# Reordering three pieces of work in a hybrid Fourier/SSD encoder layer: the transposed sums of dt, the weighted inputs, the stores of unit outputs

## The chip, the cores and the metric

The kernel runs on one core of one Trainium2 chip. The metric is the time of one execution on the device in microseconds (us). For a kernel that was run several times the median counts; a profiled execution is one more run, with a time of its own.

## The reference, cut to what matters

One encoder layer is computed for two sequences, a prompt of 1024 tokens and a sample of 2048 tokens, with 1024 features each:

```python
u = rms_norm(h, norm_w);  proj = u @ w_in            # 1024 -> 2*512 + 1536 + 2560 + 48
z_f, u_f, z_s, xbc, dt_raw = split(proj)
y_f = (fft2(u_f).real @ w_fmix) * silu(z_f)          # Fourier group
xbc = silu(depthwise_conv5(xbc) + conv_b);  xs, B, C = split(xbc)
dt = softplus(dt_raw + dt_bias)                      # 24 heads forward, 24 backward
a_cs = cumsum(dt * A) in chunks of 128 tokens
y_diag = (C B^T * exp(a_cs[l] - a_cs[s]) masked) @ (xs * dt)      # inside a chunk
states = B^T (xs * dt * exp(a_cs[-1] - a_cs));  scanned over the chunks
y_off  = C @ state_before_chunk * exp(a_cs)          # across chunks
y_s = group_norm((y_fwd + y_bwd + D * xs) * silu(z_s))
h = h + concat(y_f, y_s) @ w_out;  h = h + (p @ w_ple_in) * sigmoid(h @ w_ple_gate)
y = rms_norm(h, final_norm_w)
```

The decay exp(a_cs[l] - a_cs[s]) is needed as a 128 by 128 mask for each chunk, head and direction. To make it, the kernel lays a_cs out as rows, and each row is then loaded into all 128 partitions.

## The kernel before

The tokens are cut into three blocks of 1024: P (the prompt), S1 and S2 (the sample's halves). The first part of the kernel, up to about 1967 us of the profile, does the input projection and the whole SSD work of the three blocks; the Fourier group and the output products come behind it. The change and the prediction concern the first part alone.

**The backbone of the first part** is the projection. Its output is made in jobs of 128 columns (`Job`, line 312). A job has three pieces, one for each third of the block's tokens, and a piece is 24 matmuls on TensorE (line 361): 8 tiles of the contraction, each in three passes, since every operand is held as a rounded part and a rest. Before a job its weights are loaded (`wr`, line 182, one buffer, on the SyncE queue), rounded by ScalarE (`wh`, line 189), and the rest is taken by GpSimd (`wl`, line 190).

**The order of everything else is written out by hand.** `step` (line 286) runs one piece. Ahead of the piece it runs all entries that `pre` has put down for that step, behind it those that `post` has put down, each list in the order in which the entries were registered. Nothing is scheduled beyond that: every engine, and the SyncE queue of DMAs, takes its instructions in the order in which they are written, and waits where an operand is not there. So an entry's step says where it stands on its engine's list, and among entries of one step the order of registration says it. The older unit's entries stand first, since its plan was registered first.

**At the start of a block** the jobs for dt, the first C and the first B run. In steps counted from the block's start, `dt_sums` (line 464, behind step 13) forms the running sums of dt * A with matmuls and copies them to `acs` on ScalarE (line 471). `dt_rows` (line 486, behind step 14) turns `acs` with eight transposes on TensorE into `prw` (line 493); ScalarE copies that to `rows` and takes its exponential, `erow` (lines 494 and 495). `dt_out` (line 498, ahead of step 16) stores both to DRAM, ROWd and EXPd.

**Unit u** is two heads, 128 channels. Its x job starts at step s0, and units of a block follow each other at 9 steps, so three jobs lie between them (the last unit has 6). Unit 0 starts at step 12 of its block. In steps counted from s0, the plan (line 671) says:

- `rows_in` p = 0 to 3 (ahead of steps 4, 6, 8, 10): two DMAs each, which load rows of ROWd into all partitions (`R`, line 540, three buffers for each direction).
- `rows_cut` (ahead of 6, 8, 10, 12): GpSimd masks both `R` (line 548, two instructions). `rows_exp` (ahead of 7, 9, 11, 13): eight exponentials on ScalarE (line 558). `rows_joined` (ahead of 8, 10, 12, 14): two VectorE operations (lines 563 and 564). `diag` (behind 9, 11, 13, 15): the eight matmuls `pd` (line 575).
- `tokens` (behind 7 and 8): transposes of x into `xm` (lines 421 and 423).
- `weighted` (ahead of 8, 9, 10, 11): GpSimd multiplies `xm` by `wd` into `xw` (line 587, two buffers), one instruction for each direction and half. `states` (behind 9, 10, 11, 12): the matmuls `pst` from `xw` (line 607), then VectorE carries the state over four chunks (lines 614 and 618).
- `decays` (ahead of 11 and 13): loads of `er` from EXPd (line 635). `across` (behind 14 and 16): the matmuls `po` (line 649) and four VectorE operations into the output `y`.
- `gated` (ahead of 16 and 18): GpSimd multiplies `y` by `zT` (line 658), and in block S1 makes two products more (lines 662 and 663). `out` (ahead of 17 and 19): the store of `y` to Yd (line 667), in S1 also of `zT` to ZSd (line 669).

So steps 16 to 19 of one unit are steps 7 to 10 of the next. Beside this, from unit 2 on, `weight_sums` (line 193) forms sums of the output weights: GpSimd lines 217 to 222, its loads on line 205 and its stores to WSd on lines 227 to 229, all on the SyncE queue. While blocks P and S1 run, the next block's tokens are loaded nine times in pieces `xt` for their norm (line 122), which ScalarE squares (line 719).

Of the kernel before, what the change touches and what calls it, by code (L numbers as in the profile page):

```python
# [56 lines left out]
def tile_hybrid_encoder(ctx: ExitStack, tc: tile.TileContext, a):  # L57
# [37 lines left out]
    def bcast_rows(src, n):  # L95
        return src.partition_broadcast(n)
# [5 lines left out]
    with ExitStack() as ph:  # L102
# [63 lines left out]
        def dt_weights_in():  # L166
            wdr = sp.tile([P, KT, 64], F32, tag="R1", bufs=3, name="wdr")
            V.memset(wdr, 0.0)
            for d in range(2):
                nc.sync.dma_start(  # L170
                    wdr[:, :, 32 * d:32 * d + 24],
                    w_in[:, C_DT + 24 * d:C_DT + 24 * (d + 1)].rearrange("(k p) c -> p k c", p=P))
            return wdr

        def dt_weights(wdr):
            S.copy(wdt[:, :, 0, :], wdr)
            V.tensor_tensor(wdt[:, :, 1, :], wdr, wdt[:, :, 0, :].bitcast(F32), op=ALU.subtract)
# [100 lines left out]
        def pre(s_, fn, *args):  # L278
            assert s_ >= slot[0], (s_, slot[0])
            before.setdefault(s_, []).append((fn, args))  # L280

        def post(s_, fn, *args):
            assert s_ >= slot[0], (s_, slot[0])
            behind_.setdefault(s_, []).append((fn, args))

        def step(piece=None):
            for fn, args in before.pop(slot[0], []):
                fn(*args)
            if piece is not None:
                piece()  # L290
            for fn, args in behind_.pop(slot[0], []):
                fn(*args)
            slot[0] += 1
# [231 lines left out]
        class Unit:  # L525
# [145 lines left out]
            def plan(self, s0):  # L671

                B, g = self.B, self.g
                self.y, self.xw, self.er, self.H, self.R, self.xm = {}, {}, {}, {}, {}, {}
                if self.u % 3 == 0:
                    for k, s_ in enumerate((1, 3) if g else (4, 5)):
                        post(s0 + s_, group_tokens, B, g, 4 * k)
                    for k, s_ in enumerate((6, 7)):
                        post(s0 + s_, group_cb, B, g, 4 * k)
                for p in range(4):  # L680
                    s_ = s0 + 4 + 2 * p
                    pre(s_, self.rows_in, p)
                    pre(s_ + 2, self.rows_cut, p)
                    pre(s_ + 3, self.rows_exp, p)
                    pre(s_ + 4, self.rows_joined, p)
                    post(s_ + 5, self.diag, p)
                post(s0 + 7, self.tokens, 0)
                pre(s0 + 8, self.weighted, 0, 0)
                post(s0 + 8, self.tokens, 4)
                pre(s0 + 6, self.state_in)  # L690
                pre(s0 + 9, self.weighted, 1, 4)
                post(s0 + 9, self.states, 0, 0)
                pre(s0 + 10, self.weighted, 0, 4)
                post(s0 + 10, self.states, 1, 4)
                pre(s0 + 11, self.weighted, 1, 0)
                post(s0 + 11, self.states, 0, 4)
                post(s0 + 12, self.states, 1, 0)
                for d in (1, 0):
                    pre(s0 + 11, self.decays, d, 0)
                    pre(s0 + 13, self.decays, d, 4)  # L700
                post(s0 + 14, self.across, 0)
                pre(s0 + 16, self.gated, 0)
                pre(s0 + 17, self.out, 0)
                post(s0 + 16, self.across, 4)
                pre(s0 + 18, self.gated, 4)
                pre(s0 + 19, self.out, 4)

        def norm_piece(b, i):

# [14 lines left out]
        def ple_weights():  # L724
            nc.sync.dma_start(PLd, a["w_ple_in"][0].rearrange("(k p) c -> p k c", p=P))
# [36 lines left out]
        def x_in(b, i):  # L762
            xs[b["n"], i] = load_x(b, i)

        def x_norm(b, i):
            x_normed(b, i, xs[b["n"], i])

        def x_turn(b, i):
            x_turned(b, i, xs.pop((b["n"], i)))
# [5 lines left out]
        with tc.manual_schedule():  # L775
            b0 = BLOCKS[0]
            x_in(b0, 0)
            nc.sync.dma_start(nwb, bcast_rows(a["norm_w"][0], P))
            x_in(b0, 1)
            x_in(b0, 2)  # L780
            coming[0].load()
            x_in(b0, 3)
            wdr = dt_weights_in()
            x_in(b0, 4)
            x_norm(b0, 0)
            x_norm(b0, 1)
            x_turn(b0, 0)
            x_norm(b0, 2)
            x_turn(b0, 1)
            coming[0].split()  # L790
            coming[1].load()
            x_in(b0, 5)
            x_norm(b0, 3)
            x_turn(b0, 2)
            dt_weights(wdr)
            coming[1].split()
            pre(0, small_in)
            post(2, small_constants)
            for i in range(3, 9):
                if i > 3:  # L800
                    pre(i - 4, x_norm, b0, i)
                if i > 5:
                    pre(i - 6, x_in, b0, i)
                post(i - 3, x_turn, b0, i)
            pre(9, decay_rates)
            for B, js, what in rows_:
                bi, s0 = B.bi, slot[0]
                if what == "first":
                    q = s0 if bi else s0 + 1
                    post(q + 7, dt_turned, B)  # L810
                    pre(q + 8, dt_softplus, B, 0)
                    pre(q + 9, dt_softplus, B, 1)
                    post(s0 + 13, dt_sums, B)
                    post(s0 + 14, dt_rows, B)
                    pre(s0 + 16, dt_out, B)
                elif what == "last" and bi < 2:
                    b = BLOCKS[bi + 1]
                    for i, s_ in enumerate((2, 3, 4, 4, 5, 6, 8, 9, 10)):
                        pre(s0 + (0, 0, 1, 2, 2, 3, 5, 6, 7)[i], x_in, b, i)
                        pre(s0 + s_ - 1, x_norm, b, i)  # L820
                        post(s0 + s_, x_turn, b, i)
                elif isinstance(what, int):
                    B.units[what].plan(s0)
                    if 2 <= what < 10:
                        weight_sums(8 * bi + what - 2, s0)
                    if what == 3 and bi == 1:
                        ple_weights()
                    if what == 6 and bi < 2:
                        for i in range(9):
                            pre(s0 + 2 * i, norm_piece, BLOCKS[bi + 1], i)  # L830
                for si in range(3):
                    for j in js:
                        step(lambda: j.piece(si))
            while before or behind_:
                step()
# [550 lines left out]
```

## Time and profile before

| what | value |
|---|---|
| median of 3 runs | 3039.06 us (3034.24 to 3042.33) |
| the profiled execution | 3031.59 us, its span 3029.8 us |
| TensorE matmul busy | 2836.0 us, 94% |
| VectorE, ScalarE, GpSimd busy | 2228.9, 1389.1, 1475.5 us |
| mean granted TensorE clock | 0.972 |
| projection matmuls, line 361 | 8640, from 21 to 1967 us |
| DMA | 440.56 MB, mean 145 GB/s |

How to read it: the profile gives one execution, instruction by instruction. A row of a timeline says when an instruction (or a run of like ones) began, how long it took, its engine, line and operands, and in brackets how long its engine had been idle before it and what ended that. A row of the waits sums such idle time by who waited for whom: total, count, longest. A busy TensorE is what one wants here, so idle time in front of its instructions is what can be gained, and idle time on the other engines counts only where TensorE comes to wait for it.

### The profile page before, as it was taken

Reading aid. Unit: us, or ns where it says so; the run is one execution under the profiler, and the core shown is the slowest. Engines: PE = TensorE matmul, PEld = TensorE weight load, DVE = VectorE, ACT = ScalarE, POOL = GpSimd, SP = SyncE. Lnnn points to the kernel's source line nnn. Section 1 sums busy time; section 2 is a strip of 40 time slices with the busy share of each in tenths; the row PEclk is TensorE's granted clock in tenths of the full one; section 3 lists DMA queues with packets and bytes.
Section 4 is the critical chain, followed back from the end, with each engine's and each line's share of the span. In section 5 each row is a group of like instructions: output and inputs, shape, how many; then the busy total and the mean of one; then the engine's idle time right before and its main releaser. Section 6 shows DMA issues by size and latency. Waiting matters only on the chain. (4 is left out here: it accounts for less than half of the span.)

```text
span 3029.8 us, 47051 instructions
## 1 busy us (share of the span) xinstructions
PE 2836.0 (94%) x17252; PEld 2566.2 (85%) x17252; DVE 2228.9 (74%) x3412; ACT 1389.1 (46%) x2980; POOL 1475.5 (49%) x1114
## 2 busy tenths in 40 slices
PE   6899999989999899989999999969999899989998
PEld 6899989988999889989999999957677677768887
DVE  3687767666687568666779787687989988875665
ACT  4444545434544454434544444434433533354554
POOL 1355645431567565642555655455777578610000
PEclk9999999999999999999999999979999999999999
DMA  3378878972588778862677787566554644352221
GB/s 96 76 129 162 158 157 173 139 142 79 125 171 167 152 181 165 154 167 64 127 154 146 159 144 158 117 210 250 173 184 132 236 149 150 133 198 91 94 85 69
DMA packets 454579, 440.56 MB, mean 145 GB/s; under 512 B 24384, under 2 KB 405444, under 8 KB 450508
## 3 DMA queue, kind: packets, MB, share of 16 engines
q1 hardware_dynamic: 454060, 436.50, 60.6%
q8 instruction: 137, 2.24, 0.3%
q14 instruction: 94, 0.77, 0.1%
q10 hardware_dynamic: 288, 1.05, 0.1%
HBM read 328.41 MB, written 110.10 MB: 145 GB/s over the span
## 5 line engine op out<-in xcount | busy, mean ns | idle before, releaser
L361 PE MATMUL ps<-uh,wh 128*128 128x342 f32 (+1 forms) x2880 | 961.6, 334 | 8.4 <-ACT uh L267 8.4
L361 PE MATMUL ps<-ul,wh 128*128 128x342 f32 (+1 forms) x2880 | 926.3, 322 | 2.5 <-DVE ul L268 2.5
L361 PE MATMUL ps<-uh,wl 128*128 128x342 f32 (+1 forms) x2880 | 927.4, 322 | 0.4 <-POOL wl L190 0.4
L190 POOL TENSOR_TENSOR wl<-wr,wh 128x1024 fp32r<-128x1024 f32 x120 | 305.5, 2546 | 707.9 <-ACT wh L189 650.5
L361 PEld LDWEIGHTS ps<-uh,wh 128*128 128x128 f32 x2880 | 552.2, 192 | 20.1 <-ACT uh L267 9.2
L361 PEld LDWEIGHTS ps<-ul,wh 128*128 128x128 f32 x2880 | 554.5, 193 | 4.2 <-DVE ul L268 3.5
L361 PEld LDWEIGHTS ps<-uh,wl 128*128 128x128 f32 x2880 | 550.4, 191 | 1.2 <-POOL wl L190 1.1
L558 ACT ACTIVATE R<-R,lb 128x128 f32<-128x128 f32 x1152 | 356.8, 391 | 98.3 <-POOL R L548 98.2
L548 POOL TENSOR_SCALAR_AFFINE_SELECT R<-R 128x512 f32<-128x512 f32 x288 | 257.5, 905 | 193.7 <-DMA R<-ROWd 187.2
L618 DVE SCALAR_TENSOR_TENSOR H<-H,cd,pst 128x64 f32<-128x64 f32 x888 | 182.6, 274 | 47.7 <-PE pst L607 44.6
L402 DVE SCALAR_TENSOR_TENSOR xT<-raw,cvt,xT 128x1024 f32<-128x1024 f32 x144 | 214.8, 1492 | 2.6
L1102 PE MATMUL X<-whP,ah 128*128 128x512 f32 x480 | 195.2, 407 | 8.0 <-ACT pu L1111 6.4
L1102 PE MATMUL X<-wlP,ah 128*128 128x512 f32 x480 | 193.6, 403 | 1.6 <-DVE wlP L861 1.6
L1102 PE MATMUL X<-whP,al 128*128 128x512 f32 x480 | 192.5, 401 | 2.4 <-DVE al L1073 2.4
L587 POOL TENSOR_TENSOR xw<-xm,wd 128x512 f32<-128x512 f32 x144 | 181.8, 1268 | 18.7 <-PE pst L607 18.5
L367 ACT COPY raw<-ps 128x342 f32<-128x342 f32 x180 | 78.3, 438 | 241.7 <-PE ps L361 226.8
L1214 POOL TENSOR_TENSOR ht<-ht,pu 128x512 f32<-128x512 f32 x96 | 151.9, 1590 | 63.1 <-ACT pu L1111 43.0
L607 PE MATMUL pst<-xw,Bm 128*128 128x128 f32 x1056 | 151.3, 285 | 24.0 <-POOL xw L587 23.8
L607 PEld LDWEIGHTS pst<-xw,Bm 128*128 128x128 f32 x1056 | 131.9, 192 | 41.6 <-POOL xw L587 30.3
L189 ACT CAST wh<-wr 128x1024 fp32r<-128x1024 f32 x120 | 125.8, 1049 | 67.9 <-DMA wr<-in_w_in 67.2
L1073 DVE TENSOR_TENSOR al<-s,ah 128x512 fp32r<-128x512 f32 x144 | 143.6, 1021 | 16.4 <-ACT ah L1072 16.3
L563 DVE TENSOR_TENSOR R<-R,R 128x512 f32<-128x512 f32 x144 | 134.1, 931 | 25.9 <-ACT R L558 23.5
(264 smaller groups left out, 5703.9 us busy)
## 6 DMA issues: line engine op xcount, KB each, us to landing
R<-ROWd SPq DMA_DIRECT2D x288, 256.0 KB
wr<-in_w_in SPq DMA_DIRECT2D x120, 512.0 KB
er<-EXPd SPq DMA_DIRECT2D x288, 128.0 KB
Hd<-ht SPq DMA_DIRECT2D x48, 512.0 KB
ht<-Hd SPq DMA_DIRECT2D x48, 512.0 KB
y<-Yd SPq DMA_DIRECT2D x46, 512.0 KB
wlP<-WSd SPq DMA_DIRECT2D x21, 1024.0 KB
Yd<-y SPq DMA_DIRECT2D x72, 256.0 KB
```

The costliest lines, as they stand in the source:

```text
L190: G.tensor_tensor(wl, raw, wh.bitcast(F32), op=ALU.subtract)
L361: T.matmul(ps[:, :n], lhsT=wt[:, kt, :], rhs=ut[:, kt, :n], start=(i == 0), stop=(i == 3 * KT - 1))
L402: V.scalar_tensor_tensor(dst, raw[:, k:k + TB], cvt[:, 20 * k + ct:20 * k + ct + 1], dst, op0=ALU.mult, op1=ALU.add)
L548: G.affine_select(out=R.rearrange("p c h l -> p (c h) l"), in_=R.rearrange("p c h l -> p (c h) l"), pattern=[[0, 4], [sgn, P]], compare_op ...
L558: S.activation(R[:, c, h, :], R[:, c, h, :], AF.Exp, bias=self.B.lb[:, 2 * p + c, hc + h:hc + h + 1])
L563: V.tensor_tensor(E[0], E[0], E[1], op=ALU.add)
L587: G.tensor_tensor(xw, self.xm[c4].rearrange("p c (h e) -> p c h e", h=2), col(self.B.wd[:, c4:c4 + 4, hc:hc + 2]).broadcast_to([P, 4, 2, 6 ...
L607: T.matmul(pst[:, c, :], lhsT=B.Bm[self.g][:, c4 + c, :], rhs=xw[:, c, :, :].rearrange("p h e -> p (h e)"), start=True, stop=True)
L618: V.scalar_tensor_tensor(dst[:, e], H[d][:, cc, e], B.cd[:, cc, hc + h:hc + h + 1], pst[:, c, e], op0=ALU.mult, op1=ALU.add)
L1073: V.tensor_tensor(al, src, ah.bitcast(F32), op=ALU.subtract)
L1102: T.matmul(ps, lhsT=at[:, k, :], rhs=wt[:, k, :], start=(first and i == 0), stop=(i == 11), skip_group_check=not first)
L1214: return lambda t: G.tensor_tensor(h, h, t, op=ALU.add)
```

## The change

Three things move; no instruction is added or taken away.

1. `dt_rows` goes from behind step 14 of a block to behind step 15. `dt_out` stays ahead of step 16.
2. In a unit's plan the loop over `rows_in`, `rows_cut`, `rows_exp`, `rows_joined` and `diag` is registered behind `tokens`, `weighted`, `states` and `decays` instead of in front of them. Their steps are the same; where both have entries in one step, the order is turned round. On GpSimd `weighted` comes ahead of `rows_cut` in steps 8 and 10; on TensorE `states` ahead of `diag` behind steps 9 and 11.
3. `out` goes from ahead of steps 17 and 19 to ahead of steps 18 and 20.

```diff
@@ plan
                     for k, s_ in enumerate((6, 7)):
                         post(s0 + s_, group_cb, B, g, 4 * k)
-                for p in range(4):
-                    s_ = s0 + 4 + 2 * p
-                    pre(s_, self.rows_in, p)
-                    pre(s_ + 2, self.rows_cut, p)
-                    pre(s_ + 3, self.rows_exp, p)
-                    pre(s_ + 4, self.rows_joined, p)
-                    post(s_ + 5, self.diag, p)
                 post(s0 + 7, self.tokens, 0)
                 pre(s0 + 8, self.weighted, 0, 0)
...
                     pre(s0 + 13, self.decays, d, 4)
+                for p in range(4):
+                    s_ = s0 + 4 + 2 * p
+                    pre(s_, self.rows_in, p)
+                    pre(s_ + 2, self.rows_cut, p)
+                    pre(s_ + 3, self.rows_exp, p)
+                    pre(s_ + 4, self.rows_joined, p)
+                    post(s_ + 5, self.diag, p)
                 post(s0 + 14, self.across, 0)
                 pre(s0 + 16, self.gated, 0)
-                pre(s0 + 17, self.out, 0)
+                pre(s0 + 18, self.out, 0)
                 post(s0 + 16, self.across, 4)
                 pre(s0 + 18, self.gated, 4)
-                pre(s0 + 19, self.out, 4)
+                pre(s0 + 20, self.out, 4)
@@ the block's start
                     post(s0 + 13, dt_sums, B)
-                    post(s0 + 14, dt_rows, B)
+                    post(s0 + 15, dt_rows, B)
                     pre(s0 + 16, dt_out, B)
```

What this does to the lists of three engines, at the places of which the prediction speaks:

ScalarE at the start of block S1, from the sums of dt on; before:

```order
L479 ACTIVATE wd<-wd 128x512
L483 ACT_TABLE_LOAD
L483 ACTIVATE lb<-lb 128x512
L367 COPY raw<-ps 128x342
L494 COPY rows<-prw 64x512
L495 ACT_TABLE_LOAD
L495 ACTIVATE erow<-prw 64x512
L494 COPY rows<-prw 64x512
L495 ACTIVATE erow<-prw 64x512
L189 CAST wh<-wr 128x1024
L406 ACTIVATE xT<-raw,cvt 128x1024
L272 ACTIVATE zT<-ps 128x342 x2
```

The same place after the change:

```order
L479 ACTIVATE wd<-wd 128x512
L483 ACT_TABLE_LOAD
L483 ACTIVATE lb<-lb 128x512
L367 COPY raw<-ps 128x342
L189 CAST wh<-wr 128x1024
L406 ACTIVATE xT<-raw,cvt 128x1024
L272 ACT_TABLE_LOAD
L272 ACTIVATE zT<-ps 128x342
L494 COPY rows<-prw 64x512
L495 ACTIVATE erow<-prw 64x512
L494 COPY rows<-prw 64x512
L495 ACTIVATE erow<-prw 64x512
```

The next job's `wh`, the start of a convolution (`xT`), and the first piece of `zT` now stand in front of the copies of the turned sums. Either list has two loads of an activation table.

GpSimd in unit 3 of block S1, from the masks of step 8 to the inputs of steps 10 and 11; before:

```order
L548 AFFINE_SELECT R_9324<-R_9324 128x512
L548 AFFINE_SELECT R_9326<-R_9326 128x512
L587 TENSOR_TENSOR xw<-xm,wd 128x512
L190 TENSOR_TENSOR wl<-wr,wh 128x1024
L658 TENSOR_TENSOR y<-y,zT 128x512
L662 TENSOR_TENSOR er_9220<-er_9220,elt 128x512
L663 TENSOR_TENSOR zT<-er_9220,zT 128x512
L587 TENSOR_TENSOR xw<-xm,wd 128x512
L548 AFFINE_SELECT R_9450<-R_9450 128x512
L548 AFFINE_SELECT R_9452<-R_9452 128x512
L587 TENSOR_TENSOR xw<-xm,wd 128x512 x2
```

The same place after the change:

```order
L587 TENSOR_TENSOR xw<-xm,wd 128x512
L548 AFFINE_SELECT R_9324<-R_9324 128x512
L548 AFFINE_SELECT R_9326<-R_9326 128x512
L190 TENSOR_TENSOR wl<-wr,wh 128x1024
L658 TENSOR_TENSOR y<-y,zT 128x512
L662 TENSOR_TENSOR er_9212<-er_9212,elt 128x512
L663 TENSOR_TENSOR zT<-er_9212,zT 128x512
L587 TENSOR_TENSOR xw<-xm,wd 128x512 x2
L548 AFFINE_SELECT R_9450<-R_9450 128x512
L548 AFFINE_SELECT R_9452<-R_9452 128x512
L587 TENSOR_TENSOR xw<-xm,wd 128x512
```

The first and the third `xw` of the unit have changed places with a pair of masks each. The second `xw` still has the same instructions in front of it: the pair of masks, the first `xw`, `wl`, and the three products of the unit before (lines 658 to 663).

The SyncE queue in the same unit, between two weight loads `wr`; before:

```order
L182 DMA wr<-in_w_in 128x8x128
L667 DMA Yd_61<-y 128x512
L669 DMA ZSd<-zT 128x512
L540 DMA R_9450<-ROWd_68 128x2x256
L540 DMA R_9452<-ROWd_68 128x2x256
L227 DMA WSd_78<-wb 128x2x256
L228 DMA WSd_78<-wb 128x256
L229 DMA WSd_78<-ws 128x4x256
L205 DMA wb<-in_w_out 128x2x256 x2
L182 DMA wr<-in_w_in 128x8x128
```

The same place after the change:

```order
L182 DMA wr<-in_w_in 128x8x128
L540 DMA R_9450<-ROWd_68 128x2x256
L540 DMA R_9452<-ROWd_68 128x2x256
L227 DMA WSd_78<-wb 128x2x256
L228 DMA WSd_78<-wb 128x256
L229 DMA WSd_78<-ws 128x4x256
L667 DMA Yd_61<-y 128x512
L669 DMA ZSd<-zT 128x512
L205 DMA wb<-in_w_out 128x2x256 x2
L182 DMA wr<-in_w_in 128x8x128
```

The two stores of the unit before now stand behind two loads of `R` and the stores of the weight sums, but still in front of the next weight load `wr`. At step 11 the second pair of stores stands in the same way behind the last pair of `R` loads and in front of the `er` loads.

## The prediction

> **What bounds the kernel now.** I read the page first, then the waits of TensorE, then the timeline of each engine around the longest of them.
>
> ```profile
> span 3029.8 us, 47051 instructions
> PE 2836.0 (94%) x17252; PEld 2566.2 (85%) x17252; DVE 2228.9 (74%) x3412; ACT 1389.1 (46%) x2980; POOL 1475.5 (49%) x1114
> ```
>
> TensorE is busy for 2836.0 of 3029.8 us, and the change takes no work from it. So only its idle time, 194 us, and the time at a low clock can be gained. The waits of TensorE, with total, count and longest, name two that the change is near:
>
> ```profile
> PE pst L607 <- POOL xw L587: 23.8, 18, 3.8
> PE prw L493 <- ACT acs L471: 17.2, 3, 7.6
> PE pd L575 <- ACT wh L189: 10.1, 2, 6.2
> ```
>
> Together 41 us, 1.4% of the span, are the most that parts 1 and 2 can win as waits. The third row matters for part 3, and so do a wait of the SyncE queue and one of ScalarE:
>
> ```profile
> SPq L667 <- POOL y L658: 243.6, 49, 9.5
> ACT xt L719 <- DMA xt<-in_x_sample: 61.0, 15, 9.1
> ```
>
> The queue stands 243.6 us in front of stores whose products GpSimd hasn't made; ScalarE waits 61.0 us for pieces of the next block's tokens.
>
> **Part 1, the transposes a step later.** The three waits are one in each block (P, S1, S2):
>
> ```profile
> 106.36 1.92 PE L493 MATMUL prw<-ident,acs 128*64 128x128 f32 x8 [7.57 <-ACT acs L471]
> 749.76 1.49 PE L493 MATMUL prw<-ident,acs 128*64 128x128 f32 x6 [4.81 <-ACT acs L471]
> 1418.40 0.85 PE L493 MATMUL prw<-ident,acs 128*64 128x128 f32 x3 [4.79 <-ACT acs L471]
> ```
>
> A step's matmuls last about 3.7 us: two groups of transposes with one step between them start 4.2 us apart, and the first takes 0.6.
>
> ```profile
> 760.73 0.60 PE L421 MATMUL ptt<-ident,BT 128*128 128x128 f32 x4
> 764.92 0.60 PE L421 MATMUL ptt<-ident,BT 128*128 128x128 f32 x4
> ```
>
> ScalarE's copy `acs` comes when it came before, so one step put into the wait leaves 3.9, 1.1 and 1.1 us. The clock adds to this. Behind the waits of S1 and S2 the granted clock (third column from the end) was low:
>
> ```profile
> 751.00:757.00 6.00, 6.00 (x29) 5.92 (x28) 1.72 (x3) 5.96 (x9) 0.00 (x0) 0.65 0.00 1
> 1420.00:1426.00 6.00, 6.00 (x28) 6.00 (x27) 1.72 (x3) 5.95 (x10) 0.00 (x0) 0.64 0.00 0
> 785.00:800.00 15.00, 13.23 (x93) 12.57 (x92) 12.27 (x20) 9.16 (x22) 12.31 (x8) 1.00 0.56 94
> 932.00:936.00 4.00, 2.70 (x11) 2.70 (x12) 2.85 (x5) 1.14 (x4) 4.00 (x4) 0.59 1.12 361
> ```
>
> 0.35 of 6 us, 2.1 us, is lost in S1 and as much in S2. The last two rows are for scale: a wait of 1.77 us (row below) left the clock at 1.00, one of 3.77 us (quoted in part 2) took it to 0.59. So 1.1 us should cost no clock, 3.9 us still should. TensorE then stands 3.7 us earlier in P, 3.7 + 2.1 = 5.8 in S1 and S2: 15.3 us. This is the upper bound of part 1.
>
> Not all of it stays, since what unit 0 needs next doesn't move as far. ScalarE in S1 before:
>
> ```profile
> 753.77 0.58 ACT L494 COPY rows<-prw 64x512 f32<-64x512 f32 x1
> 754.35 1.28 ACT L495 ACT_TABLE_LOAD   x1
> 756.60 0.59 ACT L495 ACTIVATE erow<-prw 64x512 f32<-64x512 f32 x1
> 757.09 1.04 ACT L189 CAST wh<-wr 128x1024 fp32r<-128x1024 f32 x1
> 758.03 1.25 ACT L406 ACTIVATE xT<-raw,cvt 128x1024 f32<-128x1024 f32 x1
> 759.18 0.44 ACT L272 ACTIVATE zT<-ps 128x342 f32<-128x342 f32 x1
> ```
>
> Now `wh`, `xT`, a table load and `zT` stand ahead of the rows. From 753.8 on they take 1.04 + 1.25 + 1.28 + 0.44, and rows, erow, rows 0.58 + 0.59 + 0.58: the rows are ready at 759.6, where the last `erow` began behind them at 756.60 before. Before, that readiness was not used, as the queue shows:
>
> ```profile
> 760.64 0.37 SPq L182 DMA_DIRECT2D wr<-in_w_in  x1
> 761.06 1.10 SPq L499 DMA_DIRECT2D ROWd<-rows  x1
> 765.54 3.13 SPq L540 DMA_DIRECT2D R<-ROWd  x4
> ```
>
> The store of ROWd stood behind a weight load that waited for `wl`, hence for `wh`. Now `wh` is 3.2 us earlier, and the store goes at 759.6 instead of 761.06: 1.4 us earlier. Up to 1.5 more may come because that weight load's 512 KB have left the DMA engines by then. I take 2. The loads of `R` follow it, and behind those the next weight load, which ends the chain:
>
> ```profile
> 782.39 0.64 POOL L548 TENSOR_SCALAR_AFFINE_SELECT R<-R 128x512 f32<-128x512 f32 x1 [1.83 <-DMA R<-ROWd]
> 785.62 1.06 ACT L189 CAST wh<-wr 128x1024 fp32r<-128x1024 f32 x1 [4.93 <-DMA wr<-in_w_in]
> 786.81 2.40 POOL L190 TENSOR_TENSOR wl<-wr,wh 128x1024 fp32r<-128x1024 f32 x1 [2.77 <-ACT wh L189]
> 789.16 1.56 POOL L587 TENSOR_TENSOR xw<-xm,wd 128x512 f32<-128x512 f32 x1
> 790.77 1.16 PE L607 MATMUL pst<-xw,Bm 128*128 128x128 f32 x8 [1.77 <-POOL xw L587]
> 144.98 0.71 PE L607 MATMUL pst<-xw,Bm 128*128 128x128 f32 x4 [0.51 <-POOL xw L587]
> 1454.96 1.05 POOL L587 TENSOR_TENSOR xw<-xm,wd 128x512 f32<-128x512 f32 x1
> 1457.30 0.49 PE L607 MATMUL pst<-xw,Bm 128*128 128x128 f32 x3
> ```
>
> DMA to `wh` to `wl` to the second `xw` to `pst`: TensorE already waited here in P and S1, and in S2 it had 1.3 us to spare (1457.30 less 1456.01). So unit 0's second `pst` comes 2 us earlier in P and S1 and 3.3 in S2, 7.3 in all; the rest of the 15.3 turns into a wait for GpSimd there. In S1 that wait is some 5 us and will cost clock, about 1.3 us (the lower clock after 749.76 cost 2.1). Part 1: -6, bounds -15.3 and, if nothing of the chain moves, +1.3.
>
> **Part 2, `weighted` ahead of the masks.** Unit 3 of S1 has the longest of the 18 waits:
>
> ```profile
> 922.30 1.22 POOL L548 TENSOR_SCALAR_AFFINE_SELECT R<-R 128x512 f32<-128x512 f32 x2
> 923.49 1.05 POOL L587 TENSOR_TENSOR xw<-xm,wd 128x512 f32<-128x512 f32 x1
> ...
> 931.22 2.02 POOL L587 TENSOR_TENSOR xw<-xm,wd 128x512 f32<-128x512 f32 x1
> 933.30 2.07 PE L607 MATMUL pst<-xw,Bm 128*128 128x128 f32 x8 [3.77 <-POOL xw L587]
> ```
>
> The rows left out are `wl` and the three products of unit 2; no row of GpSimd here has idle time in brackets, and TensorE waits for the second `xw`. The change only swaps the first `xw` (1.05) with the masks (1.22); the sum in front of the second is the same, so its wait stays. I count 0, with the whole 23.8 as the far end below. What it costs: masks in steps 8 and 10 come 1 to 2 us later, and exponentials, joins and `diag` behind them. They are covered by the step between each of these stages: the long wait of `pd` quoted above names `wh`, not an exponential or a join. +0.5; were the cover gone, 36 units times two masks times 1.05 would be 76 us, which sets no bound worth keeping.
>
> The same product took 1.05 us at 923.49 and 2.02 at 931.22, so a moved `xw` may land beside other VectorE work: 0.97 us more in the eleven later units of S1, +10.7, is the bound above. The Trainium skill (GPSIMD Engine Reference, Specifications) says that GpSimd shares its SBUF interfaces with VectorE, which contends where it reads two inputs from SBUF; by it the swap would give between 0 and that 10.7, and the two durations agree with it.
>
> **Part 3, stores a step later.** In unit 3 of S1 the `R` loads of step 8 stood behind a ZSd store that waited for GpSimd:
>
> ```profile
> 910.56 0.37 SPq L182 DMA_DIRECT2D wr<-in_w_in  x1
> ...
> 922.38 0.33 SPq L669 DMA_DIRECT2D ZSd<-zT  x1
> 922.80 0.93 SPq L540 DMA_DIRECT2D R<-ROWd  x2
> ```
>
> They can now follow the weight load at 910.56, and what stands behind the stores goes up to 3 us earlier, in step 10 likewise; the last of it reaches the `xt` loads, for which ScalarE waits 61.0 us, and behind two of these waits TensorE lost 10.1 us and a low clock. I take 4 of these 10.1, bounds 0 and -13. The buffers of `y` are written again two and four steps after the later stores, which is 8 us or more of cover; without it VectorE would wait for a DMA.
>
> **The sum**, against the profiled execution's own 3031.6 us (span 3029.8 and 1.8 around it): -6 + 0.5 - 4 = -9.5, 3022.1. The three runs' median, 3039.06, lies 7.5 higher; from it the same difference gives 3029.6.
>
> **The rivals.**
>
> *A. The time in unit 0 is not taken back.* If the weight load there lands with TensorE's new place, part 1 keeps its 15.3, and with part 3 at -6 the sum is -21: 3018. Against it speaks the wait 4.93 for that very load.
>
> *B. The waits only move.* If ROWd lands no earlier (its 4.5 us up to the `R` loads grow by what it starts earlier) and the queue is bound by the transfers and not by its waits, what is left is +1 to -3: about 3038. For it speaks that the `R` loads went only at 765.54, behind a store issued at 761.06.
>
> *C. Slower: loads let go early share the DMA engines with a weight load.* In step 8 the pair of `R` loads now follows `wr` at once, where it stood 12 us behind. The four `R` loads issued at 765.54 were there by 782.39, 16.9 us, so a pair takes up to 8.4. If the engines serve both together, `wr` lands up to half of that, 4.2 us, later, and `wh`, `wl` and the second `xw` with it. In the eleven later units of S1 that is +46; less the 9.5, +37: 3076. From 0.9 us of delay a unit it eats the gain. For it: 16.9 us for four loads that the queue issued in 3.13 shows them standing at the engines. Against it: in unit 0, the last `R` was there at 782.39, the weight load behind it at 785.62.
> The Trainium skill (DMA: Bandwidth & Descriptors, Queues, rings and completion order) says that an engine takes the descriptors of a ring in order; by that rule C adds nothing, and the rows of unit 0 agree.
>
> **How the numbers follow.** About 0.3%, 9.1 us, is what a measurement of this kernel tells from no change. Forecast (-14 to -4) 0.46; A 0.20; B 0.21; C 0.13. The forecast straddles the bound: 0.25 of it beyond, 0.21 within. Faster: 0.25 + 0.20 = 0.45; the same: 0.21 + 0.20 of B = 0.41; slower: C and the rest of B, 0.14. The range takes in A to -25 (3014) and at the top +5 (3044), which is part 2 at its bound of cost and a delay of 0.3 us a unit as in C; what is left out is the rest of C and the far ends.
>
> **What would show it.** Right: `prw` waits of about 3.9, 1.1 and 1.1 us; no low clock behind them in S1 and S2; the second `pst` of unit 0 waiting 2 to 5 us; the total of `pst` behind `xw` as large as before or larger; the queue's wait in front of Yd well below 243.6; `xt` waits below 61. Wrong: `pst` waits under 12 us (part 2 or A does more than I think), `wh` waiting longer for `wr` (C), or a new wait of VectorE for a store of `y`.

## The result, and the profile after

| | before | changed |
|---|---|---|
| median, timed side by side | 3040.36 us (3034.24 to 3042.33, 4 runs) | 3018.1 us (3010.3 to 3022.51, 4 runs) |
| ratio, 95% interval | | 0.9927 (0.99 to 0.9955) |
| the profiled execution, its span | 3031.59, 3029.8 us | 3021.5, 3019.7 us |

The change makes the kernel 22 us faster, where 9.5 were forecast. The changed kernel was timed whole in this group of runs alone; in the three later groups the kernel before has medians of 3028.44, 3030.56 and 3030.88 us, so a ratio is taken within a group only. The page of the changed kernel begins:

```profile
span 3019.7 us, 47067 instructions
PE 2831.3 (94%) x17252; PEld 2570.1 (85%) x17252; DVE 2217.9 (73%) x3412; ACT 1389.5 (46%) x2980; POOL 1488.2 (49%) x1114
```

TensorE's idle time fell from 194 to 188 us and its busy time by 4.7, so this one profile explains only 10 of the 22 us. Where it was won and lost shows when the trace is cut at the last projection matmul. Columns from the left: window, its length, busy time of TensorE (and count), weight loads, VectorE, ScalarE, GpSimd, granted clock, DMA share, GB/s. Before:

```profile
0.00:1967.00 1967.00, 1858.83 (x12818) 1786.07 (x12820) 1396.88 (x2338) 918.26 (x2068) 989.08 (x772) 0.98 0.70 141
1967.00:3029.80 1062.80, 977.17 (x4436) 780.10 (x4436) 832.04 (x1074) 470.86 (x913) 486.39 (x342) 0.96 0.45 154
```

Changed:

```profile
0.00:1948.60 1948.60, 1854.44 (x12818) 1789.79 (x12819) 1383.40 (x2338) 919.58 (x2067) 997.74 (x771) 0.98 0.71 142
1948.60:3019.70 1071.10, 976.86 (x4436) 780.28 (x4434) 834.49 (x1074) 469.88 (x913) 490.48 (x343) 0.96 0.45 153
```

The first part, which the change is about, is 18.4 us shorter. The second part, whose code is the same, took 8.3 us more in this execution. Part of either difference is how executions vary: in the profile of the kernel before whose second part is left out (below), the first part ends near 1956 us, not at 1967. The rest is a question for the experiments.

The transposes `prw` of the changed kernel, one row for each block (start, duration, and in brackets the idle time and what ended it):

```profile
106.47 1.61 PE L493 MATMUL prw<-ident,acs 128*64 128x128 f32 x8 [2.62 <-ACT acs L471]
747.11 1.06 PE L493 MATMUL prw<-ident,acs 128*64 128x128 f32 x8 [1.03 <-ACT acs L471]
1402.66 1.06 PE L493 MATMUL prw<-ident,acs 128*64 128x128 f32 x8 [1.01 <-ACT acs L471]
```

17.2 us of waiting became 4.7. The clock behind the waits of S1 and S2 (third column from the end) stays full; the third row, behind the second `pst` of unit 0 in S2, does not:

```profile
748.00:754.00 6.00, 6.00 (x42) 5.98 (x41) 2.00 (x4) 5.64 (x7) 1.75 (x1) 1.00 0.02 4
1404.00:1410.00 6.00, 6.00 (x42) 5.99 (x41) 1.73 (x3) 5.95 (x7) 2.20 (x1) 1.00 0.01 3
1439.00:1445.00 6.00, 6.00 (x23) 6.00 (x24) 5.93 (x11) 2.60 (x9) 5.55 (x4) 0.51 0.66 158
```

For here part of the time is taken back. Unit 0's second `pst` in P, a new wait and the second `pst` in S1, and the second `pst` in S2:

```profile
143.07 1.16 PE L607 MATMUL pst<-xw,Bm 128*128 128x128 f32 x8 [2.41 <-POOL xw L587]
763.57 0.42 PE L361 MATMUL ps<-uh,wh 128*128 128x342 f32 x1 [2.31 <-DVE zT L273]
783.17 1.16 PE L607 MATMUL pst<-xw,Bm 128*128 128x128 f32 x8 [0.55 <-POOL xw L587]
1438.98 2.08 PE L607 MATMUL pst<-xw,Bm 128*128 128x128 f32 x8 [3.72 <-POOL xw L587]
```

The waits by who waited for whom (total, count, longest):

```profile
ACT xt L719 <- DMA xt<-in_x_sample: 58.9, 16, 9.9
ACT wh L189 <- DMA wr<-in_w_in: 56.2, 31, 6.2
PE pst L607 <- POOL xw L587: 28.6, 18, 6.9
```

`pst` waits a little more than before (23.8), ScalarE waits less for weights (67.2 before, from the full list of waits). The SyncE queue's longest waits in total, the first three:

```profile
SPq L182 <- POOL wl L190: 459.1, 97, 34.0
SPq L1142 <- PE pt L1130: 213.0, 21, 15.1
SPq L1233 <- POOL ht L1214: 184.4, 42, 14.1
```

The row of the stores to Yd, 243.6 us before, is gone from the top; it is 39.5 now. What the queue no longer waits in front of the stores it now partly waits in front of weight loads (409.3 before). In unit 3 of S1 the queue of the changed kernel reads:

```profile
898.73 0.37 SPq L182 DMA_DIRECT2D wr<-in_w_in  x1
899.25 6.11 SPq L540 DMA_DIRECT2D R<-ROWd  x2
...
910.64 1.10 SPq L667 DMA_DIRECT2D Yd<-y  x1
911.83 0.69 SPq L669 DMA_DIRECT2D ZSd<-zT  x1
```

The pair of `R` loads is issued 0.5 us behind the weight load; before it stood 12.2 us behind (922.80 less 910.56), after a store that waited for GpSimd.

### The profile page after: what moved, and what is told of

Same layout as the page of the kernel before. It is cut to its first block, busy times and chain, and to the rows that moved or that the text cites. A ratio compares the mean times of both kernels' runs of the same rounds, so it can differ in the third digit from the quotient of the medians.

```text
span 3019.7 us, 47067 instructions
## 1 busy us (share of the span) xinstructions
PE 2831.3 (94%) x17252; PEld 2570.1 (85%) x17252; DVE 2217.9 (73%) x3412; ACT 1389.5 (46%) x2980; POOL 1488.2 (49%) x1114
## 5 line engine op out<-in xcount | busy, mean ns | idle before, releaser
L190 POOL TENSOR_TENSOR wl<-wr,wh 128x1024 fp32r<-128x1024 f32 x120 | 298.9, 2491 | 712.2 <-ACT wh L189 698.6
L548 POOL TENSOR_SCALAR_AFFINE_SELECT R<-R 128x512 f32<-128x512 f32 x288 | 270.4, 954 | 117.0 <-DMA R<-ROWd 113.0
L587 POOL TENSOR_TENSOR xw<-xm,wd 128x512 f32<-128x512 f32 x144 | 188.6, 1319 | 74.1 <-ACT xm L423 62.5
L402 DVE SCALAR_TENSOR_TENSOR xT<-raw,cvt,xT 128x1024 f32<-128x1024 f32 x144 | 197.3, 1370 | 2.6
L607 PE MATMUL pst<-xw,Bm 128*128 128x128 f32 x1056 | 146.4, 281 | 28.6 <-POOL xw L587 28.6
L563 DVE TENSOR_TENSOR R<-R,R 128x512 f32<-128x512 f32 x144 | 141.3, 981 | 31.4 <-ACT R L558 28.8
L653 DVE TENSOR_TENSOR y<-y,yt 128x512 f32<-128x512 f32 (+1 forms) x144 | 154.6, 1073 | 4.9
```

The source lines that it names most:

```text
L190: G.tensor_tensor(wl, raw, wh.bitcast(F32), op=ALU.subtract)
L402: V.scalar_tensor_tensor(dst, raw[:, k:k + TB], cvt[:, 20 * k + ct:20 * k + ct + 1], dst, op0=ALU.mult, op1=ALU.add)
L548: G.affine_select(out=R.rearrange("p c h l -> p (c h) l"), in_=R.rearrange("p c h l -> p (c h) l"), pattern=[[0, 4], [sgn, P]], compare_op ...
L587: G.tensor_tensor(xw, self.xm[c4].rearrange("p c (h e) -> p c h e", h=2), col(self.B.wd[:, c4:c4 + 4, hc:hc + 2]).broadcast_to([P, 4, 2, 6 ...
L607: T.matmul(pst[:, c, :], lhsT=B.Bm[self.g][:, c4 + c, :], rhs=xw[:, c, :, :].rearrange("p h e -> p (h e)"), start=True, stop=True)
L653: V.tensor_tensor(y[:, cr], y[:, cr], t[:, cr], op=ALU.add)
```

## The experiments

The gain could come from the queue (part 3), sized too small; from the transposes (part 1), as the prediction's rival A has it; or from the second part, whose instructions a scheduler puts in order, or the variation between runs. That variation is large: one group of timings of the kernel before spans 3017.98 to 3039.63 us over 23 runs. Letters of theories are those of each run's own expectation.

### Each part alone

Only `dt_rows` moves:

```diff
-                    post(s0 + 14, dt_rows, B)
+                    post(s0 + 15, dt_rows, B)
```

> Part 1 alone (the transposes of the sums behind step 15 instead of 14; stores and order of weighted and masks as before). My theory (what unit 0 needs next does not move as far, so most of the time is taken back): 3 to 7 us less than before; the waits of prw near 2.6 to 3.9, 1.0 and 1.0 us; in P and S2 the second pst of unit 0 waits 2.4 and 3.7 us and the later jobs of these blocks start as late as before, within 1 us; in S1 4 to 5 us stay. Rival A (the time is kept): about 15 us less. Rival (the whole change works through part 1): about 20 us less.

Measured: 3026.75 us against 3028.44, ratio 0.9998 (0.9982 to 1.0014). Taken by itself, part 1 gives no gain that can be seen in the whole kernel; the interval still allows up to 5.5 us, the lower half of what was expected.

Only the loop over `rows_in` to `diag` moves behind `decays`:

```diff
-                for p in range(4):
...
                     pre(s0 + 13, self.decays, d, 4)
+                for p in range(4):
```

> Part 2 alone (weighted ahead of the masks, states ahead of diag; the rest as before). My theory (the second xw has the same work in front of it): 0 to 3 us less; the total of pst waiting for xw stays at 20 to 28 us. Rival (GpSimd no longer stands still at a mask while the first xw could run, which carries the change): 10 us or more less, and pst waiting for xw under 12 us.

Measured: 3041.83 us, ratio 1.0042 (1.0026 to 1.0058): part 2 alone is 13 us slower, against what both theories expected. The waits of `pst` for `xw` are 20.9 us in total, as the first theory has it.

Only `out` moves:

```diff
-                pre(s0 + 17, self.out, 0)
+                pre(s0 + 18, self.out, 0)
...
-                pre(s0 + 19, self.out, 4)
+                pre(s0 + 20, self.out, 4)
```

> Part 3 alone (stores of unit outputs a step later; the rest as before). My theory after the result (the queue is freed, the loads of R, of the next weights and of xt come earlier): 8 to 16 us less, the queue's wait in front of Yd far below 243.6 us, GpSimd's wait for R below 140 us (187.2 before). Rival (the queue is bound by the transfers, the waits only move): 0 to 4 us less, GpSimd's wait for R as before.

Measured: 3006.41 us, ratio 0.9935 (0.9915 to 0.9956), by the ratio 20 us. That is nearly the whole change's gain, five times what the prediction gave to part 3, and above the 8 to 16 us expected here. The queue's wait in front of Yd is 41.9 us; GpSimd's wait for `R` fell from 187.2 to 143.5, not quite to the 140 expected.

Parts 2 and 3 together (the second and the third diff):

> Parts 2 and 3 together, part 1 left as before. If the parts add up and part 1 is worth 3 to 7 us: 12 to 18 us less than before. If parts 2 and 3 need each other (R earlier is only of use when the first xw no longer stands behind the mask, or the other way round), it is 4 us or more beyond the sum of the two alone. Rival A (part 1 carries 15 us): 3 to 8 us less.

Measured: 3031.65 us, ratio 1.0004 (0.999 to 1.0018). In the whole kernel part 2 takes back all that part 3 gives, which none of the three theories has. How much of that lies in the first part this time does not tell.

Where part 2's loss lies, the two windows of its profile tell:

```profile
0.00:1956.90 1956.90, 1857.75 (x12818) 1792.11 (x12819) 1385.30 (x2338) 922.20 (x2067) 1001.83 (x771) 0.98 0.69 142
1956.90:3040.40 1083.50, 980.58 (x4437) 785.56 (x4435) 826.86 (x1074) 469.68 (x913) 480.93 (x343) 0.95 0.45 151
```

Its first part is 10 us shorter than before, its second part 20.7 us longer, with 102.9 us of idle TensorE instead of 85.6. Part 3 alone, for comparison:

```profile
0.00:1935.20 1935.20, 1849.92 (x12818) 1778.15 (x12820) 1400.70 (x2338) 916.33 (x2067) 998.65 (x772) 0.98 0.71 143
1935.20:3004.50 1069.30, 977.88 (x4437) 781.60 (x4436) 832.78 (x1074) 470.54 (x913) 489.97 (x343) 0.96 0.45 153
```

The lists of instructions show why the second parts may differ. The scheduler puts them in order, and the order that it finds is not the same for all kernels. The count is of matmuls behind the projection, out of 4152, that lie outside the longest common sequence with the kernel before (a matmul is known by its line and its operands' names, buffer numbers left out):

| kernel | out of sequence | second part in its profile |
|---|---|---|
| before | | 1062.8 us |
| part 3 alone | 0 | 1069.3 |
| the whole change | 96 | 1071.1 |
| part 1 alone | 92 | 1071.3 |
| parts 1 and 3 (next section) | 92 (the same order as part 1 alone) | 1072.3 |
| part 2 alone | 553 | 1083.5 |
| parts 2 and 3 | 553 (the same order as part 2 alone) | 1089.5 |

With one and the same order the second part took 1062.8 and 1069.3 us, so some 6 us are variation; the two kernels with 553 matmuls out of sequence lie 14 us and more above that. The 213 of the next expectation comes from another count of the same two lists.

### Parts 1 and 3, and the first part by itself

Parts 1 and 3 without part 2 (the first and the third diff above):

> Parts 1 and 3 of the change without part 2. Theory O: part 2 costs nothing in the first part; what it cost alone (ratio 1.0042) came from another order of the second part, which the scheduler chose. With part 1 the second part has nearly the order of the kernel before again (213 of 4152 TensorE instructions moved, as with part 1 alone), so this kernel should be where the whole change is: ratio 0.992 to 0.994, the second part 1063 to 1071 us in the profile. Rival W: part 2 costs its 13 us in the first part, in the whole change as well; without it the ratio falls by 0.0042 to about 0.988, and the first part ends 13 us before that of the whole change, at about 1935 us.

Measured: 2999.68 us (2994.5 to 3010.64) against 3030.56, ratio 0.9903 (0.9886 to 0.9921). The fastest whole kernel of the study, faster than before by 31 us. It lies between what O (0.992 to 0.994) and W (0.988) expect, and its interval overlaps with that of the whole change (0.9927), so by itself it decides nothing between the two. In the profiles its first part ends at 1936.3 us, 12 before that of the whole change, as W expects; its second part took 1072.3.

To take the scheduler's order out, three kernels were cut behind the first part:

```diff
+    with ExitStack() as ph:
+        zp = ph.enter_context(tc.tile_pool(name="zp", bufs=1))
+        zo = zp.tile([P, DM], F32, name="zo")
+        V.memset(zo, 0.0)
+        for s_, o in enumerate(a["out"]):
+            for i in range(8 * (s_ + 1)):
+                nc.sync.dma_start(o[i * P:(i + 1) * P, :], zo)
+    if True:
+        return
+
     R_ = dict(side="right", reuse_waits="tile")
```

> The kernel before, cut: the whole second part (Fourier group and output products) is left out, and zeros are stored to the outputs in its place. The scale for the two cut kernels beside it. Either theory: the first part ends near 1967 us as in the whole kernel, and the stores of zeros add 20 to 60 us: 1990 to 2030.

Measured: 2007.86 us (2005.89 to 2009.03).

> The changed kernel, cut in the same way: the second part left out, zeros stored. Theory O: the change's gain lies in the first part: 15 to 25 us less than the kernel before, cut (the profiles of the whole kernels had 18.4 less). Rival S: the gain came from the second part's order or from how runs vary; less than 9 us between the two cut kernels.

Measured: 1986.47 us (1985.81 to 1988.52), 21.4 us less. The ranges are far apart, and S falls: a gain as large as that of the whole kernel is there without any second part.

> Part 2 alone, cut in the same way: the second part left out, zeros stored. Theory O: the 13 us that part 2 alone cost came from the second part's order; the cut kernel is no slower than the kernel before, cut, between 10 us less and 2 us more. Rival W: part 2 costs in the first part; 10 to 15 us more than the kernel before, cut.

Measured: 2004.84 us (2003.44 to 2007.66), 3.0 us less than before. So the 13 us that part 2 alone costs in the whole kernel are not in the first part; for part 2 alone O holds and W falls. The runs of one cut kernel lie within 3 us of their median here, while the kernel before, whole, spans 3021.98 to 3035.83 in the same group; in the next group the cut kernels scatter more.

The next four were run together, the changed kernel again to link them to the three above.

> The changed kernel, cut as before (second part left out, zeros stored), once more as the scale for the next three. Either theory: 1986.5 us, give or take 2.

Measured: 1988.5 us (1982.79 to 1993.02).

> Part 3 alone, cut (second part left out, zeros stored). Theory Q: the later stores free the SyncE queue for the loads of R and bring most of the change's gain: 15 to 22 us under the 2007.9 of the kernel before, cut, so 1986 to 1993. Rival, the size that was predicted: 4 us, 2004; the rest would then have to come from parts 1 and 2 together.

Measured: 1989.23 us (1985.99 to 1992.26), 18.6 under the kernel before, cut. Q holds. The two stand in different groups; the changed kernel, cut, which is in both, differs by 2.0 us between them.

> Parts 1 and 3, cut (second part left out, zeros stored). Theory Q: part 1 keeps 4 to 6 us of unit 0 of S1 beside part 3, and part 2 is worth nothing in company: 4 to 6 us under part 3 alone, cut, and within 3 us of the changed kernel, cut (1984 to 1989). Rival A of the prediction: part 1 keeps its 15 us. Rival W: part 2 costs in company; this kernel is 5 us or more under the changed kernel, cut.

Measured: 1979.55 us (1975.19 to 1984.23): 9.7 under part 3 alone, more than Q's 4 to 6 and less than A's 15; and 7 to 9 under the changed kernel (1986.47 and 1988.5), as W has it. So part 2, worth 3 us by itself, costs 7 to 9 beside the other two. As ratios to the whole kernel before: part 3 0.6564 (0.6551 to 0.6578), parts 1 and 3 0.6533 (0.6517 to 0.6549), all three 0.6561 (0.6545 to 0.6577). The intervals of the last two just overlap, so the cost of part 2 is less sure than the gain of part 1.

What the second part costs in each kernel follows by subtraction. All numbers are ratios to the whole kernel before, timed in the same group:

| kernel | whole | cut | difference |
|---|---|---|---|
| before | 1 | 0.6628 | 0.3372 |
| part 3 alone | 0.9935 | 0.6564 | 0.3371 |
| parts 1 and 3 | 0.9903 | 0.6533 | 0.3370 |
| the whole change | 0.9927 | 0.6557, 0.6561 | 0.3370, 0.3366 |
| part 2 alone | 1.0042 | 0.6618 | 0.3424 |

Four kernels agree within 2 us, although up to 96 matmuls stand in another order. With the order of part 2 alone it costs 0.0052 more, 16 us, give or take some 6 by the intervals.

The last one also puts a unit's second `weighted` ahead of the older unit's `gated` in the same step:

```diff
-                pre(s0 + 9, self.weighted, 1, 4)
+                es = before.setdefault(s0 + 9, []); es.insert(next((k for k, e in enumerate(es) if e[0].__name__ == "gated"), len(es)), (self.weighted, (1, 4)))
```

> Parts 1 and 3, cut in the same way, and the second weighted input of a unit (step 9) put ahead of the older unit's products of the same step on GpSimd (lines 658 to 663). Theory X, that these products and the order of the masks make the second pst wait, as the prediction has it: the waits of pst for xw, some 20 us in total, fall below 8, and the kernel is 8 to 15 us faster than parts 1 and 3, cut. Rival: the waits of pst hang on the weights wl in front of both, and the older unit's products are then missed elsewhere; within 4 us.

Measured: 1979.73 us (1969.17 to 1984.52), no different. The waits of `pst` and of `wh` with parts 1 and 3, cut:

```profile
ACT wh L189 <- DMA wr<-in_w_in: 41.2, 19, 4.4
PE pst L607 <- POOL xw L587: 18.7, 15, 3.2
```

And with the second input in front of the older unit's products:

```profile
ACT wh L189 <- DMA wr<-in_w_in: 70.0, 29, 7.6
PE pst L607 <- POOL xw L587: 17.4, 12, 2.8
```

The total hardly moves. Sorted by which of a unit's four `pst` groups waits, the second falls from 11.6 to 4.1 us, while the first and the third together rise from 7.1 to 13.3. Theory X falls: putting the second input first moves the wait to the other `pst` groups. The later products also hold their stores, as the rival says: the queue's wait in front of Yd rises from 32.1 to 41.7 us, and ScalarE's for the weights from 41.2 to 70.0.

## Why the prediction was right or wrong

**Direction and size.** The forecast straddled the bound, and the result lies clearly beyond it, inside the stated range but outside the forecast's own -14 to -4. By the cut kernels the sum reads: part 3, 2007.9 to 1989.2, -18.6; part 1 beside it, -9.7; part 2 beside both, +7 to +9 (forecast: -4, -6, +0.5). The step that failed is the size of part 3. Part 2 costs where it was counted at nearly nothing, and that error hides part of the first. So it is luck that the number is that of rival A (3018): A's reason held in part only (9.7 of 15.3 us), and three misses of some 15, 4 and 7 us partly cancel.

**Part 1: the waits as worked out; what is kept about as said in sum, but not block by block.** The waits of S1 and S2 came out at 1.03 and 1.01 us for 1.1, that of P at 2.62 for 3.9 (TensorE waits another 0.92 in front of the step that was put in), and the clock behind the first two stayed at 1.00. Unit 0's second `pst` takes the time back in P and S2, with 2.41 and 3.72 us; in S1 TensorE waits 2.31 for a new reason, `zT` on VectorE, and then only 0.55. How much is kept shows in the starts of jobs (72 matmuls of line 361 each), changed less before, in us:

| place | ahead of `prw` | between `prw` and unit 0's second `pst` | behind that |
|---|---|---|---|
| P, jobs 4, 7, 10 | +0.1 | -3.8 | -0.3 |
| S1, jobs 43, 46, 52 | -2.6 | -8.9 | -7.3 |
| S2, jobs 82, 85, 88 | -15.8 | -22.3 | -15.5 |

Of some 17 us gained at the transposes about 5 are left, all of them in S1, in this profile. The same table between the cut kernels with part 3 and with parts 1 and 3 leaves 2.7, 3.1 and 2.9 in the three blocks, 9 us: what of the time is taken back varies between executions and with what else has moved. The forecast had 2, 2 less 1.3 for the clock, and 3.3. Part 1 alone leaves 0.0, 4.6 and 3.2 in its profile, and its first part ends at 1950.3 us; yet the whole kernel shows nothing (0.9998). The new order of its second part is not the reason, since parts 1 and 3 have the same order and pay nothing for it (0.3370 in the table above). Part 1 alone was not timed with the second part left out, so this stays open.

**Part 2: the second input still waits, as said; but its wait grows.** `pst` waits 28.6 us for `xw`, no less than 23.8; of the 28.6, 28.1 stand before a unit's second group. Beside parts 1 and 3 it waits longer with part 2 than without. Parts 1 and 3, whole (28.6 with part 2):

```profile
PE pst L607 <- POOL xw L587: 21.7, 11, 5.9
```

The whole change, cut (18.7 without part 2, and 22.7 in the second profile with it):

```profile
PE pst L607 <- POOL xw L587: 25.8, 14, 7.0
```

That is 4 to 7 us more. With part 2 alone the same wait falls, from 23.8 to 20.9 us in the whole kernels and from 19.6 to 15.3 in the cut ones. Both signs are those of the first part's time: 3 us gained alone, 7 to 9 lost in company.

The prediction held that "the sum in front of the second is the same". That is true of the work, but it missed a wait: `weighted` needs `xm`, ScalarE's copy of the transposes, and now the masks, and all that follows up to the second input, stand behind it while GpSimd waits for that copy. The groups of exponentials, masks and weighted inputs (busy time and mean ns of one; idle time before them, and what ended it), before:

```profile
L558 ACT ACTIVATE R<-R,lb 128x128 f32<-128x128 f32 x1152 | 356.8, 391 | 98.3 <-POOL R L548 98.2
L548 POOL TENSOR_SCALAR_AFFINE_SELECT R<-R 128x512 f32<-128x512 f32 x288 | 257.5, 905 | 193.7 <-DMA R<-ROWd 187.2 <-DVE y L653 2.2 <-DMA HFd<-hend 1.4
L587 POOL TENSOR_TENSOR xw<-xm,wd 128x512 f32<-128x512 f32 x144 | 181.8, 1268 | 18.7 <-PE pst L607 18.5
```

Parts 1 and 3, whole kernel:

```profile
L558 ACT ACTIVATE R<-R,lb 128x128 f32<-128x128 f32 x1152 | 355.9, 393 | 51.5 <-POOL R L548 51.3
L548 POOL TENSOR_SCALAR_AFFINE_SELECT R<-R 128x512 f32<-128x512 f32 x288 | 264.3, 931 | 148.5 <-DMA R<-ROWd 140.4 <-DVE raw L334 6.2 <-DVE y L653 1.9
L587 POOL TENSOR_TENSOR xw<-xm,wd 128x512 f32<-128x512 f32 x144 | 188.0, 1311 | 24.9 <-PE pst L607 18.4 <-ACT xm L423 6.4
```

The whole change:

```profile
L558 ACT ACTIVATE R<-R,lb 128x128 f32<-128x128 f32 x1152 | 356.1, 391 | 89.5 <-POOL R L548 88.0 <-DMA wr<-in_w_in 1.4
L548 POOL TENSOR_SCALAR_AFFINE_SELECT R<-R 128x512 f32<-128x512 f32 x288 | 270.4, 954 | 117.0 <-DMA R<-ROWd 113.0 <-DVE yt L652 4.0
L587 POOL TENSOR_TENSOR xw<-xm,wd 128x512 f32<-128x512 f32 x144 | 188.6, 1319 | 74.1 <-ACT xm L423 62.5 <-PE pst L607 10.7 <-DMA wr<-in_w_in 0.9
```

Parts 1 and 3 halve ScalarE's wait for masks, from 98.2 to 51.3 us; with part 2 it is 88.0 again, and GpSimd stands 62.5 us for `xm`. But TensorE does not come to wait for the later exponentials and joins: `pd` waits 3.2 us for them with parts 1 and 3, cut, and none with the whole change, cut. So the cost is at `pst`, which was counted 0, and not behind the masks, where the +0.5 stood. It fits that part 2 costs nothing alone: there the `R` loads come late anyway, and GpSimd's waits for `R` and `xm` together are 187.2 us before and 176.6 with part 2 alone, but 146.8 with parts 1 and 3 and 175.5 with the whole change. That these waits make the 7 to 9 us is argued from the rows; no run kept the swap and took the wait for `xm` away. The mean `xw` rose from 1268 to 1319 ns, 7 us over 144. By the Trainium skill's rule on shared interfaces (GPSIMD Engine Reference, Specifications) it would be between 0 and the 10.7 of the prediction, and the 7 us lie in that range; but parts 1 and 3 without the swap have 1311, so the swap is not what makes the difference.

The second thing that the prediction did not have is the scheduler. It said that part 2 moves GpSimd's and TensorE's lists in the first part; it did not look at what the same edit does to the order behind it. Part 2 alone wins 3.0 us in the first part and loses 13 in the whole kernel. Beside part 1 another order comes out, near that of before, and the loss is not seen. That the order causes it follows from the two tables above: only the kernels with 553 matmuls out of sequence have the long second part, and by subtraction it is 16 us. It was not tried by giving one kernel's order to another.

**Part 3: mechanism right, size wrong.** "I take 4 of these 10.1, bounds 0 and -13" counted only the two stalls of `pd` behind `wh`, and only 4 us of them. With part 3 alone both are gone, all 10.1 us; between the cut kernels the same row goes from 9.9 us to none, and 1.7 us of waiting for `wh` turn up at the projection. That is the largest fall among TensorE's waits in either pair, so the named path (stores, queue, `xt`, `wh`, `pd`) was right and was worth its whole price. The rest, and what the prediction did not follow, comes from other waits behind the queue: with part 3 alone GpSimd's wait for `R` loads falls from 187.2 to 143.5 us, ScalarE's for masks from 98.2 to 51.7, for weights from 67.2 to 37.5, and for `xt` from 61.0 to 50.8. Most of it happens in S1, where each half of a unit has two stores that wait for three products. TensorE's waits before, from the 43rd job to the 82nd:

```profile
PE pst L607 <- POOL xw L587: 17.4, 11, 3.8
PE pd L575 <- ACT wh L189: 6.2, 1, 6.2
PE pd L575 <- ACT R L558: 2.7, 2, 2.5
```

Part 3 alone, the same jobs, where `pd` waits for nothing:

```profile
PE pst L607 <- POOL xw L587: 11.6, 7, 4.5
```

The time, the busy time and the clock of this stretch, before:

```profile
720.00:1374.00 654.00, 610.90 (x4198) 585.22 (x4197) 466.93 (x779) 303.50 (x682) 370.97 (x285) 0.97 0.72 153
```

Part 3 alone, the same jobs:

```profile
713.00:1347.00 634.00, 606.84 (x4194) 582.11 (x4194) 474.95 (x779) 302.17 (x682) 379.83 (x284) 0.98 0.76 158
```

20 us less, 16 of them idle time (43.1 to 27.2) and 4 busy time, at a granted clock of 0.98 instead of 0.97. Between the cut kernels the same jobs take 652.3 and 634.7 us, with 45.9 and 27.0 of idle time. Of the smaller waits, that of `pst` falls in this pair too (17.1 to 14.8), though its total over the first part does not (19.6 to 22.2). The bound of -13 was too near, since it was taken from the named waits and their clock alone.

**The rivals.** A's 15.3 us did not stay: 9.7 by the cut kernels. B, that waits only move, fails by the ratio. C, that early `R` loads delay the weights, fails by the sign named for it: ScalarE's wait for `wr` fell from 67.2 to 56.2 us, although the `R` loads stand right behind the weight load. When `wr` itself lands the trace does not tell. The Trainium skill's rule of order in a ring (DMA: Bandwidth & Descriptors, Queues, rings and completion order) gives C nothing, and this agrees. No wait of VectorE for a store of `y` appeared in the first part.

## What to carry to other kernels

A wait at the head of an in-order queue is paid by everything behind it. So follow the loads behind a store that is moved out of the way to every wait of the bounding engine, and count a wait whole unless something is seen to take it back: here the one stall that was named gave 10 us of 18.6, of which 4 were counted. The queue's own 243.6 us is no measure of the gain either. When an instruction is moved ahead of another on an in-order engine, look for what it waits for itself, since that wait now belongs to all that stands behind it. And where a part of a program is put in order by a scheduler, compare its order too when only another part was edited, and time the parts by themselves.

## What was not expected of the hardware

Four `er` loads, issued one after another, held the SyncE queue for 3.3 us at one place and 10.5 at the next, of which the first load took 7.9, as the changed kernel's queue in the middle of S1 shows:

```profile
1020.46 3.33 SPq L635 DMA_DIRECT2D er<-EXPd  x4
1024.27 0.30 SPq L122 DMA_DIRECT2D xt<-in_x_sample  x1
1026.19 0.59 SPq L182 DMA_DIRECT2D wr<-in_w_in  x1
1026.83 10.52 SPq L635 DMA_DIRECT2D er<-EXPd  x4
```

Nothing else is issued in that time. ScalarE then waits for the piece of tokens `xt`, and the weights behind it wait too:

```profile
1040.06 1.06 ACT L719 ACTIVATE xt<-xt 114x1024 f32<-114x1024 f32 x1 [9.89 <-DMA xt<-in_x_sample]
1042.55 1.04 ACT L189 CAST wh<-wr 128x1024 fp32r<-128x1024 f32 x1 [0.65 <-DMA wr<-in_w_in]
```

The same place before had 8.5 us for the four `er` loads, 8.6 us of waiting for `xt`, and then the longer of the two stalls of `pd`, 6.16 us; in the changed kernel `pd` still waits 3.26 there. So `xt` waits came down only from 61.0 to 58.9 us. The time that the queue takes to issue a load is a cost of its own here: none of the moved stores stands between these loads, and the profile shows no wait of the queue for an engine among them. What held the issue is not shown.
